# A two-layer decoder trunk: the recurrent mixer's chunks ordered by hand on four engines

## The chip, the cores and the metric

The kernel runs on one core of a Trainium2 chip. The metric is the device time of one execution, in microseconds (us). Times of "before" are the median of 3 runs, 2150.8 us (2145.18 to 2152.62). The engines are called as in the profile: PE is TensorE (PEld its weight loads), DVE VectorE, ACT ScalarE, POOL GpSimd, SP the engine whose queue issues most DMAs. One line of a timeline merges neighbouring instructions of one kind (x8: eight of them); a bracket at its end gives the idle time of the engine just before it and what ended that.

## The reference

x is 1024 tokens by 1024 features. Layer 0 mixes tokens with an mLSTM (4 heads, keys of 96, values of 192) beside a cross-attention over 256 memory tokens; one input projection feeds both, one output projection takes both. A SwiGLU feed-forward follows. Layer 1 does the same with a sliding-window attention. The change is in the mLSTM of layer 0:

```python
scores = einsum('bhcjd,bhcsd->bhcjs', qc, kc) * exp(dmat - m_row[..., None])   # decay mask, causal
num = einsum('bhcjs,bhcsv->bhcjv', scores, vc) + inter_w[..., None] * einsum('bhcjk,bhcvk->bhcjv', qc, C_st)
den = sum(scores, -1) + inter_w * einsum('bhcjk,bhck->bhcj', qc, n_st)
h = num / maximum(abs(den), exp(-m_row))[..., None]
C_new = decay * C + einsum('bhl,bhlv,bhlk->bhvk', w, v_c, k_c)                 # state, chunk after chunk
hm = hm * rsqrt(mean(hm * hm, -1) + EPS) * g_out * sigmoid(o)                  # norm per head, gate
```

The result does not depend on the length of a chunk; the kernel takes 128 tokens, so 8 chunks.

## The kernel before

All of it is one function, `trunk`, built with a scheduler that sets each engine's order and the semaphores. The program advances a nominal time with every matrix product that it emits (`line.now`). Side work is written as generators that `yield` a nominal delay; `line.poll` after each group of products emits what is due, and `line.need(key)` emits all that is left of a key. The scheduler may then move instructions against each other on an engine; inside `tc.manual_schedule` the written order of the named engines is kept.

Layer 0 starts with the memory's keys and values, then the input projection in six groups of columns (`ogm`, `q`, `k`, `v0`, `v1`, `o`; products `pa_...`). The weights of each group come in by SP's queue (`wa_k_raw`), ScalarE casts the high part (`wa_k_hi`, L237) and VectorE takes the rest (L238). During `q` the memory attention of the eight tiles runs as side work, and `gate_chain` computes the gates' running sums and maxima, from which come `iw`, `negm`, `ws`, `dec` and `ucol`; the row part of the decays goes to device memory (`r_spill`, 32 rows of 128). The sigmoid gates `o` are spilled too (`o_spill`).

Then comes the mixer, `mlstm_chunk(c)` (L1228). For each chunk of 128 tokens and 4 heads:

- SP loads the row decays, one row broadcast to all partitions (`dm`, L1233), POOL builds the weighted keys (`kw`, L1239) and adds the causal mask (L1246), ACT takes the exponential (L1257).
- PE transposes queries and keys (`pqk`), DVE and ACT copy one half each out of PSUM (`qkT`, L1254).
- PE multiplies scores (`psc`), DVE multiplies them by the decays (`sc`, L1262).
- PE multiplies keys by values, the growth of the state (`pu`), and DVE adds it to the decayed state (`state`, L1277).
- PE multiplies queries by the state before this chunk (`pi`) and scores by values (`pn`). ACT scales the first by `iw` (`num`, L1296), DVE adds the second (L1302).
- The norm: DVE forms the normaliser `den` in three small operations, a reciprocal last (L1312 to L1314); ACT takes the sum of squares of `num` times `den` (L1317, output `junk`); DVE, POOL (a power, L262) and DVE make the factor `r`; DVE multiplies values, factor and output gate into the page `v` (L1323).

Two chunks are alive at a time: chunk c starts chunk c + 2 after its sums. `dm`, `kw`, `qkT`, `state`, `num` have two buffers each, and `og`, the loaded gate, lies in the five shared pages (`xpage`). PSUM has eight banks, taken in turn.

`OutProjection.all` follows: it transposes pages 0, 4, 1 and 5 (`pt_mix`), ACT and DVE split each into two parts (`f`, L283 and L284), and the first products (`po`) use tiles 0 and 4, then 1 and 5; tiles 2, 6, 3 and 7 are transposed later. The weights' split parts are stored to device memory (`wst`) by SP. After that the feed-forward and layer 1 follow, with products in orders written by hand.

Of the kernel before, what the change touches and what calls it, by code (L numbers as in the profile page):

```python
# [9 lines left out]
F32 = mybir.dt.float32  # L10
# [110 lines left out]
def trunk(ctx: ExitStack, tc: tile.TileContext, a: dict, out: bass.AP):  # L121
# [430 lines left out]
    class OutProjection:  # L552
# [72 lines left out]
        def all(self, pages, first, early):  # L625
# [564 lines left out]
    for (nm, c0, n), after in zip(groups, groups[1:] + [None]):  # L1190
        for t0 in range(0, NT, 2):
# [27 lines left out]
    mneg = tp.tile([P, P], F32, name="mneg")  # L1219
    pool.memset(mneg, 0.0)  # L1220
    pool.affine_select(
        out=mneg, in_=mneg, pattern=[[1, P]], base=0, channel_multiplier=-1, compare_op=ALU.is_ge, fill=NEG
    )

    states = {}
    iw, nm_, ws, dec, ucol = (g_sb[n] for n in ("iw", "negm", "ws", "dec", "ucol"))

    def mlstm_chunk(c):  # L1228
        ck = slice(c * P, (c + 1) * P)
        va = vs[c][:, MEM_W:].rearrange("p (h d) -> p h d", h=HEADS)  # L1230

        dm = tp.tile([P, HEADS, P], F32, tag="dm", bufs=2, name=f"dm_{c}")
        nc.sync.dma_start(  # L1233
            out=dm.rearrange("p h n -> p (h n)"),
            in_=rd[c * HEADS : (c + 1) * HEADS, :].rearrange("h n -> (h n)").partition_broadcast(P),
        )
        if c < NT - 1:
            kw = tp.tile([P, HEADS, DQK], F32, tag="kw", bufs=2, name=f"kw_{c}")
            pool.tensor_tensor(  # L1239
                out=kw,  # L1240
                in0=qk[:, c, QK_W:].rearrange("p (h d) -> p h d", h=HEADS),
                in1=ws[:, c].unsqueeze(2).to_broadcast([P, HEADS, DQK]),
                op=ALU.mult,
            )
        yield 2.5 if c < 2 else 0.5
        pool.tensor_tensor(out=dm, in0=dm, in1=mneg.unsqueeze(1).to_broadcast([P, HEADS, P]), op=ALU.add)  # L1246

        qkT = tp.tile([DQK, 2, HEADS, P], F32, tag="qkT", bufs=2, name=f"qkT_{c}")
        for j in range(2):
            p = ps(f"pqk_{c}_{j}")  # L1250
            for h in range(HEADS):
                o = j * QK_W + h * DQK
                flip(p[:DQK, h * P : (h + 1) * P], qk[:, c, o : o + DQK])
            (act.copy if j else dve.tensor_copy)(qkT[:, j].rearrange("p h n -> p (h n)"), p[:DQK, :])  # L1254
        yield 1
        for h in range(HEADS):
            act.activation(dm[:, h], dm[:, h], AF.Exp, bias=ucol[:, c, h : h + 1])  # L1257
        psc = ps(f"psc_{c}")
        for h in range(HEADS):
            mm(psc[:, h * P : (h + 1) * P], qkT[:, 1, h], qkT[:, 0, h], True, True)  # L1260
        sc = tp.tile([P, HEADS, P], F32, tag="sc", bufs=2, name=f"sc_{c}")
        dve.tensor_tensor(out=sc, in0=psc.rearrange("p (h n) -> p h n", h=HEADS), in1=dm, op=ALU.mult)  # L1262

        if c < NT - 1:
            state = states.get(c - 1)
            new = states[c] = tp.tile([DQK, HEADS, DVA], F32, tag="state", bufs=2, name=f"state_{c}")
            for j in range(2):
                pu = ps(f"pu_{c}_{j}")
                for e_ in range(2):
                    h = 2 * j + e_  # L1270
                    mm(pu[:DQK, e_ * DVA : (e_ + 1) * DVA], kw[:, h], va[:, h], True, True)
                if c == 0:
                    dve.tensor_copy(new[:, 2 * j : 2 * j + 2].rearrange("p e d -> p (e d)"), pu[:DQK, : 2 * DVA])
                    continue
                for e_ in range(2):
                    h = 2 * j + e_
                    dve.scalar_tensor_tensor(  # L1277
                        out=new[:, h],
                        in0=state[:, h],
                        scalar=dec[:DQK, c, h : h + 1],  # L1280
                        in1=pu[:DQK, e_ * DVA : (e_ + 1) * DVA],
                        op0=ALU.mult,
                        op1=ALU.add,
                    )
        yield 2
        og = xpage(f"og_{c}")[:, :V_W]
        nc.sync.dma_start(out=og, in_=od[ck, :])
        num = tp.tile([P, HEADS, DVA], F32, tag="num", bufs=2, name=f"num_{c}")
        for j in range(2):
            nv = num[:, 2 * j : 2 * j + 2].rearrange("p e d -> p (e d)")  # L1290
            if c:
                pi = ps(f"pi_{c}_{j}")
                for e_ in range(2):
                    h = 2 * j + e_
                    mm(pi[:, e_ * DVA : (e_ + 1) * DVA], qkT[:, 0, h], states[c - 1][:, h], True, True)
                    act.mul(num[:, h], pi[:, e_ * DVA : (e_ + 1) * DVA], iw[:, c, h : h + 1])  # L1296
            pn = ps(f"pn_{c}_{j}")
            for e_ in range(2):
                h = 2 * j + e_
                mm(pn[:, e_ * DVA : (e_ + 1) * DVA], sc[:, h], va[:, h], True, True)  # L1300
            if c:
                dve.tensor_tensor(out=nv, in0=pn[:, : 2 * DVA], in1=nv, op=ALU.add)  # L1302
            else:
                dve.tensor_copy(nv, pn[:, : 2 * DVA])
            yield 0.5
        if c + 2 < NT:
            line.run(mlstm_chunk(c + 2), "mlstm")
        yield 0.5

        den, ss = (small([P, HEADS], n, bufs=2) for n in ("den", "ssh"))  # L1310
        dn = num[:, :, DV]
        dve.scalar_tensor_tensor(out=den, in0=dn, scalar=-1.0, in1=dn, op0=ALU.mult, op1=ALU.max)  # L1312
        dve.tensor_tensor(out=den, in0=den, in1=nm_[:, c], op=ALU.max)
        dve.reciprocal(den, den)  # L1314
        junk = xp.tile([P, 1024], BF16, tag="junk", bufs=1, name="junk")[:, :DV]
        for h in range(HEADS):
            act.activation(junk, num[:, h, :DV], AF.Square, scale=den[:, h : h + 1], accum_out=ss[:, h : h + 1])  # L1317
        yield 2
        r = rsqrt_mean(ss, DV, f"h_{c}", HEADS)
        dve.tensor_tensor(out=r, in0=r, in1=den, op=ALU.mult)  # L1320
        for h in range(HEADS):
            s = slice(h * DV, (h + 1) * DV)
            dve.scalar_tensor_tensor(  # L1323
                out=vs[c][:, MEM_W + h * DV : MEM_W + (h + 1) * DV],
                in0=num[:, h, :DV],
                scalar=r[:, h : h + 1],
                in1=og[:, s],
                op0=ALU.mult,
                op1=ALU.mult,
            )  # L1330
# [303 lines left out]
```

## Time and profile before

| | us |
|---|---|
| median of 3 runs (lowest, highest) | 2150.8 (2145.18, 2152.62) |
| the profiled execution | 2148.25 |
| its span, first to last instruction | 2146.5 |
| PE busy in the span | 2090.9 |
| from the first `pqk` to the first `po` | 295.29 to 369.76 |

All starts in the prediction are us from the span's first instruction. A busy time with its count divided gives the duration of one; where equal instructions follow each other without a gap, the start of the next row less the start of this gives what they cost the engine, since neighbours overlap a little. In the chain of waits each row holds only what that piece adds to the path.

### The profile page before, as it was taken

What the parts mean: (1) busy time and instruction counts of PE and PEld (TensorE: products, weight loads), DVE (VectorE), ACT (ScalarE), POOL (GpSimd) and SP (SyncE); (2) the same over time, 40 slices, a digit from 0 to 9 for tenths busy, and PEclk for the clock granted to TensorE, in tenths of its full rate; (3) what the DMA queues carried; (4) which work ended last, traced back from release to release, by engine and by line L of the source; (5) the groups of instructions that cost most, each with busy time, mean ns of one, the idle gap of its engine ahead of it and who ended that gap; (6) DMA issues with size and microseconds to landing.
All of it is one profiled execution on the core that took longest, in us unless ns stands there. A gap on an engine that the chain in (4) does not pass through costs nothing.

```text
span 2146.5 us, 30078 instructions
## 1 busy us (share of the span) xinstructions
PE 2090.9 (97%) x10628; PEld 1773.4 (83%) x10628; DVE 1281.9 (60%) x2449; ACT 1099.8 (51%) x2345; POOL 173.1 (8%) x277
## 2 busy tenths in 40 slices
PE   8999987999999999999999999999999999999998
PEld 7899977888888888888888888988888888888886
DVE  6332237577675766664585337757767667665556
ACT  6542236565545545354475336646555454544544
POOL 1000032022000000000012111001300000000002
PEclk9999998999999999999999999999999999999999
DMA  6111253693453544566674004049445445357667
GB/s 214 44 31 39 77 195 100 227 324 131 159 170 133 185 144 157 197 226 200 196 244 116 24 21 158 2 173 325 169 132 183 141 161 169 132 171 251 193 192 244
DMA packets 197814, 340.63 MB, mean 159 GB/s; under 512 B 23880, under 2 KB 79776, under 8 KB 197664
## 3 DMA queue, kind: packets, MB, share of 16 engines
q1 hardware_dynamic: 195360, 334.53, 47.1%
q10 hardware_dynamic: 2304, 4.20, 0.6%
q8 instruction: 83, 1.36, 0.3%
q14 instruction: 67, 0.55, 0.1%
HBM read 231.16 MB, written 104.35 MB: 156 GB/s over the span
## 4 chain that ended last, share of the span: by engine, by line
PE 79%; DVE 5%; issue 4%; ACT 3%; DMA 2%; POOL 1%; POOLq 0%; SPq 0%; DVEq 0%; ACTq 0%
PE fuu L186 11%; PE fgu L186 11%; PE fou L186 8%; PE po L186 7%; PE fud L186 6%; PE fgd L186 5%; PE fod L186 5%; PE foc L186 3%; PE fuc L186 3%; PE fgc L186 3%; PE pb_mq L186 2%; PE pb_q L186 2%; PE pa_v L186 2%; PE pov L186 2%; PE pa_k L186 2%
## 5 line engine op out<-in xcount | busy, mean ns | idle before, releaser
L944 DVE TENSOR_TENSOR so_lo<-so,so_hi 128x512 fp32r<-128x512 f32 x308 | 201.1, 690 | 156.3 <-ACT so_hi L943 156.1
L943 ACT CAST so_hi<-so 128x512 fp32r<-128x512 f32 x308 | 177.8, 619 | 196.3 <-PE fou L186 75.8
L186 PE MATMUL po<-wout_hi,f 128*128 128x512 f32 x512 | 162.0, 395 | 6.4 <-DVE f L284 6.4
L262 POOL TENSOR_TENSOR r<-v,neghalf 128x1 f32<-128x1 f32 (+1 forms) x76 | 59.2, 784 | 1099.0 <-DVE v L260 1070.0
L186 PE MATMUL fou<-so_lo,so_hi 128*128 128x512 f32 x352 | 137.3, 391 | 0.2
L186 PE MATMUL fou<-so_hi,so_lo 128*128 128x512 f32 x352 | 136.9, 389 | 0.0
L186 PE MATMUL fou<-so_hi,so_hi 128*128 128x512 f32 x352 | 135.2, 390 | 0.8 <-ACT so_hi L943 0.8
L186 PEld LDWEIGHTS po<-wout_hi,f 128*128 128x128 f32 x512 | 97.3, 190 | 26.7 <-DVE f L284 6.6
L186 PE MATMUL po<-wout_lo,f 128*128 128x512 f32 x256 | 100.8, 394 | 0.0
L186 PEld LDWEIGHTS fou<-so_lo,so_hi 128*128 128x128 f32 x352 | 66.1, 188 | 15.6 <-DVE so_lo L944 2.1
L186 PEld LDWEIGHTS fou<-so_hi,so_hi 128*128 128x128 f32 x352 | 66.0, 188 | 14.9 <-ACT so_hi L943 1.2
L186 PEld LDWEIGHTS fou<-so_hi,so_lo 128*128 128x128 f32 x352 | 66.1, 188 | 13.4
L699 ACT ACTIVATE wg<-wg,gcols 128x256 f32<-128x256 f32 x160 | 66.4, 499 | 13.5 <-DMA wg<-in_w_ffn_in 13.5
L710 DVE TENSOR_TENSOR t1u_lo<-wu,t1u_hi 128x512 fp32r<-128x512 f32 x22 | 15.2, 692 | 94.4 <-ACT t1u_hi L709 94.4
L186 PE MATMUL fod<-so_hi,so_hi 128*128 128x512 f32 x176 | 68.5, 389 | 0.0
L186 PE MATMUL fod<-so_lo,so_hi 128*128 128x512 f32 x176 | 68.5, 389 | 0.0
L186 PE MATMUL fod<-so_hi,so_lo 128*128 128x512 f32 x176 | 68.5, 389 | 0.0
L699 ACT ACTIVATE wu<-wu,gcols 128x256 f32<-128x256 f32 x160 | 66.5, 500 | 0.8 <-DMA wu<-in_w_ffn_in 0.8
L186 PE MATMUL pa_v<-wa_v_hi,h 128*128 128x384 f32 (+1 forms) x256 | 66.2, 339 | 0.0
L720 DVE TENSOR_TENSOR wo_raw<-wo_raw,wo_raw 128x512 f32<-128x512 f32 x88 | 60.6, 688 | 1.5
L186 PE MATMUL fgu<-f,t2g_hi 128*128 128x512 f32 (+1 forms) x176 | 53.5, 387 | 5.4 <-ACT gx L786 5.4
L186 PE MATMUL fuu<-f,t2u_hi 128*128 128x512 f32 x176 | 56.7, 403 | 0.3
(462 smaller groups left out, 5721.6 us busy)
## 6 DMA issues: line engine op xcount, KB each, us to landing
so<-sp SPq DMA_DIRECT2D x154, 256.0 KB, 3.1
wg<-in_w_ffn_in SPq DMA_DIRECT2D x44, 512.0 KB, 3.6
wo_raw<-in_w_ffn_out SPq DMA_DIRECT2D x88, 256.0 KB, 3.5
wu<-in_w_ffn_in SPq DMA_DIRECT2D x44, 512.0 KB, 4.2
tp<-wo_raw SPq DMA_DIRECT2D x88, 256.0 KB, 2.7
so<-tp SPq DMA_DIRECT2D x88, 256.0 KB, 3.3
so<-in_w_ffn_out SPq DMA_DIRECT2D x66, 256.0 KB, 3.7
sp<-ux SPq DMA_DIRECT2D x22, 512.0 KB, 3.8
```

Source lines behind the costliest of these rows:

```text
L186: pe.matmul(o, lhsT=lhsT, rhs=rhs, start=start, stop=stop, **kw)
L262: pool.tensor_tensor(out=r, in0=v, in1=neghalf[:, :width], op=ALU.pow)
L699: act.activation(v, v, AF.Copy, scale=g)
L710: dve.tensor_tensor(out=lo, in0=v, in1=h.bitcast(F32), op=ALU.subtract)
L720: dve.tensor_tensor(out=r[o], in0=r[x_], in1=r[y_], op=ALU.add)
L943: act.copy(h, v)
L944: dve.tensor_tensor(out=lo, in0=v, in1=h.bitcast(F32), op=ALU.subtract)
```

## The change

The mixer becomes a loop of ten rounds, i from -2 to 7, inside `tc.manual_schedule` for PE, DVE, ACT and POOL. A round holds four chunks at once: transposes of chunk i + 2, scores and state of i + 1, sums of i, norm of i - 1, and the gates of i - 2 (two heads each in its middle and at its end). Loads and masks run ahead: the decays of i + 4 are loaded, those of i + 3 masked, those of i + 2 exponentiated. Buffers grow to three (`qkT`, `state`, `num`, `og`) and four (`dm`, `den`, `ssh`); `og` and `num` have pages of their own except in the last two chunks.

The norm loses its reciprocal: ACT squares `num` itself, and the factor is (mean of squares + EPS den²) to the power -1/2. The third small operation on `den` is now EPS den² (L1362 of the changed kernel), and the two around the power become one ahead of it (L1371).

The memory attention gets a pool of its own, which is given back after the `v1` columns; the mask and the four `dm` buffers take that room, and decays of chunks 0 to 2 are written there (`first_decays`). The norms of the last two chunks are side work (`m_end`, key "ends"), needed before `keep(0)` in the output projection.

```diff
@@ OutProjection.all
             self.tiles(0, (0, 4))
+            line.need("ends")
             self.keep(0)
...
+    def first_decays():
+        for c in range(4):
+            decay_load(c)
+        yield 6
+        for c in range(3):
+            decay_mask(c)
+            if c < 2:
+                state_keys(c)
+            yield 1.5
+            if c < 2:
+                decay_exp(c)
...
-    line.need("gates", "mem0")
+        elif nm == "v1":
+            line.need("gates", "mem0")
+            mem_cm.__exit__(None, None, None)
...
+            line.run(first_decays(), "decay", 4)
+    line.need("decay")
...
-        dve.reciprocal(den, den)
+        dve.scalar_tensor_tensor(out=den, in0=den, scalar=EPS, in1=den, op0=ALU.mult, op1=ALU.mult)
...
+    def m_scale(c):
+        den, ss = vals[c]
+        dve.scalar_tensor_tensor(out=den, in0=ss, scalar=1.0 / DV, in1=den, op0=ALU.mult, op1=ALU.add)
+        pool.tensor_tensor(out=ss, in0=den, in1=neghalf[:, :HEADS], op=ALU.pow)
...
+    def m_end(c):
+        yield 1
+        for h in range(HEADS):
+            m_square(c, h)
+        yield 2
+        m_scale(c)
+        yield 1.5
+        m_gate(c, range(HEADS))
+
+    with tc.manual_schedule(engines={mybir.EngineType[e] for e in ("PE", "DVE", "Activation", "Pool")}):
+        pn1 = None
+        for i in range(-2, NT):
+            ends = 0 <= i - 1 < NT - 2
+            if 0 <= i < NT:
+                m_load(i)
+            if 4 <= i + 4 < NT:
+                decay_load(i + 4)
+            flips = m_flip(i + 2) if i + 2 < NT else None
+            if pn1:
+                m_add(i - 1, 1, pn1)
+            if flips:
+                dve.tensor_copy(*flips[0])
+            if i >= 1:
+                m_normaliser(i - 1)
+            if 0 <= i - 2 < NT - 2:
+                m_gate(i - 2, (0, 1))
+            if 0 <= i + 1 < NT:
+                psc = m_scores(i + 1)
...
+            if ends:
+                m_square(i - 1, 0)
+            if flips:
+                act.copy(*flips[1])
+            if ends:
+                for h in range(1, HEADS):
+                    m_square(i - 1, h)
+            if 0 <= i + 1 < NT - 1:
+                m_state(i + 1, m_growth(i + 1))
+            if ends:
+                m_scale(i - 1)
+            if 2 <= i + 2 < NT - 1:
+                state_keys(i + 2)
+            if i >= 0:
+                if 3 <= i + 3 < NT:
+                    decay_mask(i + 3)
+                pi, pn = m_sums(i, 0)
+                if pi:
+                    m_scaled(i, 0, pi)
+                m_add(i, 0, pn)
+                if i + 2 < NT:
+                    decay_exp(i + 2, (0, 1))
...
+            if 0 <= i - 2 < NT - 2:
+                m_gate(i - 2, (2, 3))
+        m_add(NT - 1, 1, pn1)
+        m_normaliser(NT - 1)
+        m_gate(NT - 3, range(HEADS))
+    for c in (NT - 2, NT - 1):
+        line.run(m_end(c), "ends", 0.5 + c - NT + 2)
```

What this makes of the engines' order is shown at three places. The first is DVE in the middle of the mixer; `v` is the page that the gates write, `num` the sums, `sc` the decayed scores. Before:

```order
L1302 TENSOR_TENSOR num_3008<-pn_0_3014,num_3008 128x386
L1277 SCALAR_TENSOR_TENSOR state_2986<-state_2955,dec,pu_0_2987 96x193 x2
L1277 SCALAR_TENSOR_TENSOR state_2986<-state_2955,dec,pu_1_2992 96x193 x2
L1302 TENSOR_TENSOR num_3008<-pn_1_3023,num_3008 128x386
L1302 TENSOR_TENSOR num_3029<-pn_0_3035,num_3029 128x386
L1312 SCALAR_TENSOR_TENSOR den<-num_3008 128x4
L1313 TENSOR_TENSOR den<-den,negm 128x4
L1314 RECIPROCAL den<-den 128x4
L1302 TENSOR_TENSOR num_3029<-pn_1_3048,num_3029 128x386
L1254 COPY qkT_3063<-pqk_0_3064 96x512
```

and in one round of the change:

```order
L1352 TENSOR_TENSOR num_2979<-pn_1_3049,num_2979 128x386
L1408 COPY qkT_3063<-pqk_0_3064 96x512
L1360 SCALAR_TENSOR_TENSOR den<-num_2979 128x4
L1361 TENSOR_TENSOR den<-den,negm 128x4
L1362 SCALAR_TENSOR_TENSOR den<-den 128x4
L1378 SCALAR_TENSOR_TENSOR v_616<-num_2903,ssh,og_2902 128x192 x2
L1416 TENSOR_TENSOR sc_3088<-psc_3083,dm_2855 128x512
L1321 SCALAR_TENSOR_TENSOR state_3105<-state_3025,dec,pu_0_3099 96x193 x2
L1321 SCALAR_TENSOR_TENSOR state_3105<-state_3025,dec,pu_1_3100 96x193 x2
L1371 SCALAR_TENSOR_TENSOR den<-ssh,den 128x4
L1352 TENSOR_TENSOR num_3059<-pn_0_3118,num_3059 128x386
L1378 SCALAR_TENSOR_TENSOR v_616<-num_2903,ssh,og_2902 128x192 x2
```

Where two chunks' steps stood next to each other, every round now has each step once, with four chunks' buffers side by side.

The second place is ACT ahead of the `k` columns; `mpT` belongs to the memory attention's last tile, `qk` is the copied projection. Before:

```order
L492 COPY mpT_7_1_1599<-mpt_7_1_1594 128x512
L237 ACTIVATE wa_k_hi<-wa_k_raw,gcols 128x384 x4
L1173 COPY qk<-pa_q_1558 128x384
L237 ACTIVATE wa_k_hi<-wa_k_raw,gcols 128x384
L1173 COPY qk<-pa_q_1559 128x384
```

and in the change:

```order
L492 COPY mpT_7_1_1602<-mpt_7_1_1597 128x512
L237 ACTIVATE wa_k_hi<-wa_k_raw,gcols 128x384 x3
L1175 ACTIVATE dm_2520<-dm_2520,ucol 128x128
L237 ACTIVATE wa_k_hi<-wa_k_raw,gcols 128x384
L1213 COPY qk<-pa_q_1561 128x384
L237 ACTIVATE wa_k_hi<-wa_k_raw,gcols 128x384
L1213 COPY qk<-pa_q_1562 128x384
L1175 ACTIVATE dm_2520<-dm_2520,ucol 128x128 x3
L1175 ACTIVATE dm_2522<-dm_2522,ucol 128x128 x4
```

The exponentials of chunks 0 and 1 (`dm_2520`, `dm_2522`), written in the program behind the `v1` columns, stand here, the first of them between the sixth and the seventh cast of the `k` weights; on SP their loads stand ahead of the v weights.

The third place is DVE at the mixer's end; `v_903` is chunk 5's page, `v_1069` chunk 6's, `v_1066` and `v_1074` chunks 6 and 7 of before. Before:

```order
L260 TENSOR_SCALAR v_3375<-ssh 128x4
L1320 TENSOR_TENSOR r_3377<-r_3377,den 128x4
L1323 SCALAR_TENSOR_TENSOR v_1066<-num_3315,r_3377,og_3313 128x192 x4
L260 TENSOR_SCALAR v_3384<-ssh 128x4
L1320 TENSOR_TENSOR r_3386<-r_3386,den 128x4
L1323 SCALAR_TENSOR_TENSOR v_1074<-num_3327,r_3386,og_3325 128x192 x4
L284 TENSOR_TENSOR f_3400<-pt_mix_0_0_3401,f_3400 128x512
```

and in the change:

```order
L1352 TENSOR_TENSOR num_3339<-pn_1_3361,num_3339 128x386
L1371 SCALAR_TENSOR_TENSOR den<-ssh,den 128x4
L1360 SCALAR_TENSOR_TENSOR den<-num_3339 128x4
L1361 TENSOR_TENSOR den<-den,negm 128x4
L1378 SCALAR_TENSOR_TENSOR v_1069<-num_3292,ssh,og_3291 128x192
L1362 SCALAR_TENSOR_TENSOR den<-den 128x4
L1378 SCALAR_TENSOR_TENSOR v_903<-num_3217,ssh,og_3216 128x192 x4
L1371 SCALAR_TENSOR_TENSOR den<-ssh,den 128x4
L1378 SCALAR_TENSOR_TENSOR v_1069<-num_3292,ssh,og_3291 128x192 x2
L284 TENSOR_TENSOR f_3387<-pt_mix_0_0_3388,f_3387 128x512
```

Chunk 7's gates now come after the `f` subtractions of pages 0, 4, 1 and 5. Chunk 5's four gates appear here although the round before had them already: the loop's last round has i - 2 = 5, and the line after the loop issues them once more. Behind these rows each engine's order is that of before.

More of the change, by code (lines that the diff above doesn't have):

```diff
@@ L1218, in trunk @@
     tp = tp0.pool
[L1219 to L1235, printed above, removed]
-        )
[L1237 to L1248, printed above, removed]
@@ new lines, in trunk, with m_load, m_flip @@
+    qkTs, scs_, states, nums, ogs, vals = {}, {}, {}, {}, {}, {}
+    def m_load(c):
+        late = c >= NT - 2
+        ogs[c] = xpage(f"og_{c}")[:, :V_W] if late else tp.tile([P, V_W], F32, tag="og", bufs=3, name=f"og_{c}")
+        nums[c] = (
+            xpage(f"num_{c}")[:, : HEADS * DVA]
+            if late
+            else tp.tile([P, HEADS * DVA], F32, tag="num", bufs=3, name=f"num_{c}")
+        )
+        nc.sync.dma_start(out=ogs[c], in_=od[c * P : (c + 1) * P, :])
+    def m_flip(c):
+        qkT = qkTs[c] = tp.tile([DQK, 2, HEADS, P], F32, tag="qkT", bufs=3, name=f"qkT_{c}")
+        pqk = [ps(f"pqk_{c}_{j}") for j in range(2)]
@@ L1249, in mlstm_chunk @@
         for j in range(2):
-            p = ps(f"pqk_{c}_{j}")
             for h in range(HEADS):
                 o = j * QK_W + h * DQK
[L1253 to L1257, printed above, removed]
+                flip(pqk[j][:DQK, h * P : (h + 1) * P], qk[:, c, o : o + DQK])
@@ L1264, in mlstm_chunk @@
[L1264 to L1288, printed above, removed]
-        for j in range(2):
[L1290 to L1297, printed above, removed]
+        return psc
@@ L1311, in mlstm_chunk, with m_sums @@
-        dn = num[:, :, DV]
+                dve.scalar_tensor_tensor(
+                    out=new[:, h],
+                    in0=states[c - 1][:, h],
+                    scalar=dec[:DQK, c, h : h + 1],
+                    in1=pus[j][:DQK, e_ * DVA : (e_ + 1) * DVA],
+                    op0=ALU.mult,
+                    op1=ALU.add,
+                )
+    def m_sums(c, j):
+        va, sc, qkT, pi = m_values(c), scs_[c], qkTs[c], None
+        if c:
+            pi = ps(f"pi_{c}_{j}")
+            for e_ in range(2):
+                h = 2 * j + e_
+                mm(pi[:, e_ * DVA : (e_ + 1) * DVA], qkT[:, 0, h], states[c - 1][:, h], True, True)
+        pn = ps(f"pn_{c}_{j}")
+        for e_ in range(2):
+            h = 2 * j + e_
+            mm(pn[:, e_ * DVA : (e_ + 1) * DVA], sc[:, h], va[:, h], True, True)
+        return pi, pn
@@ new lines, in m_scaled, with m_add, m_normaliser @@
+    def m_scaled(c, j, pi):
+        for e_ in range(2):
+            h = 2 * j + e_
+            act.mul(nums[c][:, h * DVA : (h + 1) * DVA], pi[:, e_ * DVA : (e_ + 1) * DVA], iw[:, c, h : h + 1])
+    def m_add(c, j, pn):
+        v = nums[c][:, 2 * j * DVA : 2 * (j + 1) * DVA]
+        if c:
+            dve.tensor_tensor(out=v, in0=pn[:, : 2 * DVA], in1=v, op=ALU.add)
+        else:
+            dve.tensor_copy(v, pn[:, : 2 * DVA])
+    def m_normaliser(c):
+        den = small([P, HEADS], "den", bufs=4)
+        dn = nums[c].rearrange("p (h d) -> p h d", h=HEADS)[:, :, DV]
```

89 lines of the change are left out of this document (65 added, 24 removed).

## The prediction

> **What bounds the kernel now.** The page comes first: TensorE is busy for nearly the whole span, so only what shortens TensorE's own row of work, or its waits, counts.
>
> ```profile
> span 2146.5 us, 30078 instructions
> PE 2090.9 (97%) x10628; PEld 1773.4 (83%) x10628; DVE 1281.9 (60%) x2449; ACT 1099.8 (51%) x2345; POOL 173.1 (8%) x277
> ```
>
> The profiled execution took 2148.25 us, 1.75 us more than its span. The change touches the recurrent mixer, so I cut its stretch out by windows: from the first chunk's transposes to the fifth score product (L186, `psc`), on to the ninth, and on to the first product of the output projection. Columns: stretch, its length, busy time (and instructions) of PE, PEld, DVE, ACT, POOL, granted clock, DMA share, GB/s.
>
> ```profile
> 295.29:317.44 22.15, 15.57 (x90) 13.90 (x88) 10.77 (x22) 11.10 (x32) 11.47 (x12) 0.85 0.86 296
> 317.44:349.58 32.14, 27.37 (x161) 25.91 (x161) 24.92 (x68) 19.68 (x64) 12.21 (x11) 0.89 0.41 136
> 349.58:369.76 20.18, 12.61 (x91) 11.72 (x89) 13.97 (x46) 13.53 (x44) 4.04 (x4) 0.95 0.24 78
> ```
>
> Here no engine is full: PE is busy 55.55 of 74.47 us, and at a granted clock of 0.85 to 0.95. PE's timeline gives the milestones and the long waits.
>
> ```profile
> 295.29 1.04 PE L193 MATMUL pqk<-ident,qk 128*96 128x128 f32 x8
> ...
> 299.65 1.04 PE L193 MATMUL pqk<-ident,qk 128*96 128x128 f32 x8
> 304.70 2.08 PE L186 MATMUL psc<-qkT 96*128 96x128 f32 x8 [4.01 <-ACT qkT L1254]
> ...
> 317.44 1.16 PE L186 MATMUL psc<-qkT 96*128 96x128 f32 x8 [0.51 <-ACT qkT L1254]
> ...
> 349.58 1.12 PE L186 MATMUL psc<-qkT 96*128 96x128 f32 x8
> ...
> 369.76 0.80 PE L186 MATMUL po<-wout_hi,f 128*128 128x512 f32 x1 [6.35 <-DVE f L284]
> ```
>
> Three stretches: 22 us until chunk 2's scores; then four chunks (2 to 6) in 32.14 us, 8.0 us each; then 20 us to the projection, of which the last 6.35 us are a wait for chunk 7's norm.
>
> **The change, part by part.** Its instructions are almost those of before; their order is new. So I price a round of the new order on each engine, then follow the path. VectorE's starts, row to next row, are the cost of each operation:
>
> ```profile
> 333.62 0.68 DVE L1254 COPY qkT<-pqk 96x512 f32<-96x512 f32 x1
> 334.22 0.15 DVE L1313 TENSOR_TENSOR den<-den,negm 128x4 f32<-128x4 f32 x1
> ...
> 350.79 0.69 DVE L1262 TENSOR_TENSOR sc<-psc,dm 128x512 f32<-128x512 f32 x1 [0.31 <-PE psc L186]
> 351.40 1.39 DVE L1277 SCALAR_TENSOR_TENSOR state<-state,dec,pu 96x193 f32<-96x193 f32 x4
> 352.71 0.16 DVE L260 TENSOR_SCALAR v<-ssh 128x4 f32<-128x4 f32 x1
> ...
> 354.20 1.41 DVE L1323 SCALAR_TENSOR_TENSOR v<-num,r,og 128x192 f32<-128x192 f32 x4
> 355.52 0.17 DVE L260 TENSOR_SCALAR v<-ssh 128x4 f32<-128x4 f32 x1
> ...
> 358.33 1.02 DVE L1302 TENSOR_TENSOR num<-pn,num 128x386 f32<-128x386 f32 x2
> 359.38 0.17 DVE L1312 SCALAR_TENSOR_TENSOR den<-num 128x4 f32<-128x4 f32 x1
> ...
> 360.07 1.03 DVE L1302 TENSOR_TENSOR num<-pn,num 128x386 f32<-128x386 f32 x2
> ```
>
> Copy 0.60, score 0.61, four state updates 1.31, four gates 1.32, two adds 1.05, three small normaliser operations 0.69, and the new scale step, of the small ones' kind, 0.2: 5.8 us a round on VectorE. TensorE's price is in the chain of waits, where it runs back to back.
>
> ```profile
> 347.99 1.75 PE pqk L193 x16
> 349.74 0.96 PE psc L186 x8
> 350.70 1.32 PE pu L186 x8
> ```
>
> Eight transposes are 0.88, scores 0.96, growth 1.32; the two sums have 193 columns like growth, so I take 1.32 for each: 5.8 us too. ScalarE:
>
> ```profile
> 302.90 1.28 ACT L1257 ACTIVATE dm<-dm,ucol 128x128 f32<-128x128 f32 x4
> ...
> 359.62 0.75 ACT L1296 ACTIVATE num<-pi,iw 128x193 f32<-128x193 f32 x2 [0.37 <-PE pi L186]
> 360.27 0.44 ACT L1317 ACTIVATE junk<-num,den 128x192 bf16<-128x192 f32 x1
> ...
> 360.84 0.46 ACT L1317 ACTIVATE junk<-num,den 128x192 bf16<-128x192 f32 x1
> ```
>
> A square costs 0.57 (360.27 to 360.84), two scalings 0.65, four exponentials 1.28, a copy about as VectorE's: 2.3 + 1.3 + 1.3 + 0.6 = 5.5 us. With three engines at 5.5 to 5.8, a round without any collision is about 5.9. But GpSimd works in every round, and the trace shows who collides with it:
>
> ```profile
> 324.65 1.26 POOL L1246 TENSOR_TENSOR dm<-dm,mneg 128x512 f32<-128x512 f32 x1 [0.17 <-POOL r L262]
> ...
> 336.36 0.83 POOL L1239 TENSOR_TENSOR kw<-qk,ws 128x384 f32<-128x384 f32 x1 [7.48 <-PE pu L186]
> ...
> 338.66 1.16 POOL L262 TENSOR_TENSOR r<-v,neghalf 128x4 f32<-128x4 f32 x1 [0.36 <-DVE v L260]
> ```
> ```profile
> 324.72 2.40 DVE L1323 SCALAR_TENSOR_TENSOR v<-num,r,og 128x192 f32<-128x192 f32 x4
> ...
> 338.54 1.41 DVE L1323 SCALAR_TENSOR_TENSOR v<-num,r,og 128x192 f32<-128x192 f32 x4
> ```
>
> Four gates that began just behind a mask (`dm`, 1.26 us) took 2.40 instead of 1.41: the first stood still until the mask ended. Beside a power (`r`) they took their 1.41. So I count the mask as a stop for VectorE's operations that read SBUF alone (normaliser, gates), and the power as none. In the new order GpSimd does power, keys, mask after each scale step: 1.02 + 0.83 + 1.26, with three hand-overs of 0.07 (quoted below) 3.3 us after the scale. VectorE meanwhile has an add, two gates, an add and a copy, 0.5 + 0.66 + 0.5 + 0.6 = 2.3, and comes to the normaliser 1.0 early. It then needs 0.69 + 0.66 (gates) + 0.61 + 1.31 + 0.2 = 3.5 to the next scale. Round: 3.3 + 3.5 = **6.8 us**.
>
> The Trainium skill (SBUF — State Buffer, § Who interferes with whom) says that a VectorE instruction with two SBUF inputs contends with any GpSimd instruction that reads SBUF, the first to start holding the pair to its end. For the mask the trace agrees (2.40 against 1.41); for the power the 338.54 row does not show it (1.41). By that rule the power too would stop two gates.
>
> Now the path. **Lead-in**: chunk 0's and 1's masks and exponentials have moved ahead of the mixer, so after the unchanged point 299.65 (growth of chunk 0 done, next transposes) round 0 needs only PE's 0.88 + 0.96 + 1.32 + 1.32 = 4.5, to 304.1, and chunk 2's scores start at 305.0 instead of 317.44: **-12.4**. The table load of ScalarE falls into round 0, where chunk 2's exponentials are not needed before 306. **Rounds**: four chunks at 6.8 instead of 32.14 in all: 27.2, **-4.9**. They reach chunk 6's scores at 332.2; the last scale step before the end phase (chunk 4's) is at 335.4, 3.2 behind. **End**: add, gates, add 1.7 (337.1); ScalarE's four squares of chunk 5 2.3 (339.4); scalings of chunk 6 and VectorE's add, with two gates between, 2.5 (341.9); then in the order in which ScalarE holds them two squares 1.2, two scalings 0.65, two squares 1.2, two scalings 0.65 and the add 0.5 (346.1). VectorE: scale 0.2, power with hand-overs 1.1, one gate of chunk 6 and its neighbour 0.4, four gates of chunk 5 that the change issues a second time 1.3, scale of chunk 7 0.2, two gates 0.7, the first `f` subtraction 0.7: 350.7, and the projection starts at 350.8. From chunk 6's scores that is 18.6 instead of 20.18: **-1.6**. Of the chain that ended the stage before, the last norm's power and gates no longer stand there:
>
> ```profile
> 362.76 0.07 issue
> 362.83 1.02 POOL r L262
> ...
> 366.88 1.42 DVE v L1323 x4
> ```
>
> The reciprocal was one small operation and is replaced by one: nothing. Chunk 7's power and gates go behind the `f` evictions, under the first projection pair; were that cover gone, they would cost 1.0 + 1.4 = 2.4. SP's queue now carries three decay loads ahead of the v weights and a fourth among them, and ScalarE's queue one exponential ahead of the last two `wa_k` casts:
>
> ```profile
> 144.42 1.75 PE mpo L186 x16
> ...
> 150.39 33.28 PE pa_k L186 x192
> ```
> ```profile
> DMA to landing us min/median/max: 3.2/4.1/6.0
> ```
>
> The load waits for the memory attention's end (146.2), lands by 152.2 at the slowest row of decays, mask and exponential 1.7, cast and subtraction 1.3: 155.2. PE needs that seventh slice after 36 of the 192 products of 0.173: 156.6. So I take 0, with a slack of 1.4; each us of landing beyond that costs one. In the mixer a load has more than a round, 7 us or more against 6.0, before its mask: 0. An earlier load frees nothing that PE waits for under `pa_k`, so this part has no gain; its bounds are 0 and +2.
>
> Sum: -12.4 - 4.9 - 1.6 = -18.9. On the profiled 2148.25 that gives 2129.3; the median of the three runs, 2150.8, is 2.5 above it, so I forecast a median of **2131.9**.
>
> **The rivals.** (a) The pace of before returns: rounds stay at 8.0, since each engine's queue now waits in a fixed order. Against it: each mask and exponential now stands a round or more ahead of its score; for it: VectorE was already 24.92 of 32.14 busy. Four rounds cost 4.8 more: 2136.7. (b) The power stops the gates too. Two gates then wait from 0.5 after the scale to 1.1, and push keys and mask: 0.6 a round, 2.4: 2134.3. The Trainium skill page above is the ground for that rule; the 338.54 row speaks against. (c) The change does not do what it says: the decays, once moved under the k columns, hold ScalarE's casts there, and TensorE waits as long as it gains. That takes landings of some 25 us against 6.0: about 2150. (d) Slower: the granted clock. Where PE waits 4.01, eight scores took 2.08 instead of 0.96. If rounds with waits keep the clock at half, a round is PE's 11.6: five of them, 24 more; lead-in and last rounds add 10: 2166. It decides once about 25 of these 34 come true. Against it, the middle stretch held 0.89 with PE busy for 85%, which the new round equals.
>
> No collision at all, rounds of 5.9, gives -3.6: 2128.3. That is the forecast's own lower end, 8.0 the upper.
>
> **How the numbers follow.** Forecast 0.70, (a) 0.15, (b) 0.08, (c) 0.04, (d) 0.03. Runs of this kernel lie from 2145.18 to 2152.62, so 0.3%, 6.5 us, is about what can be told from no change; faster are the first three cases, 0.93, the same is (c), slower (d). The range goes from 2128.3 less the 5 that spread and a shorter end allow, 2123, to (a) with 2 for the loads and 2 for the spread, 2141.
>
> **What would show it.** In the changed profile: chunk 2's scores 9.7 us after the first transposes, not 22; score rows 6.8 apart; gates or normaliser of over 1 us beside a mask, none beside a power; the first projection product 55.5 us after the first transposes, with a wait of 3 to 7; and no new wait in `pa_k`. Wrong would be score rows 8 or more apart, a granted clock under 0.8 in the rounds, or a gap before `pa_k` or `pa_v`.

## The result and the profile after

The changed kernel takes 2125.38 us (median of 4 runs, 2124.24 to 2130.15), the kernel before, run beside it, 2151.62 (4 runs, 2145.18 to 2152.62). The ratio is 0.9896, with a 95% interval of 0.9879 to 0.9912 (the quotient of the two medians is 0.9878): faster by about 1%, against a forecast of 2131.9 with a range of 2123 to 2141. Its profiled execution took 2125.09 us, 23.2 less than the 2148.25 of before, where the sum of the prediction had 18.9 less.

The page of the changed kernel, as before: TensorE has 10.3 us less of busy time (2080.6 against 2090.9) with as many instructions; 7.8 of them are gone from the mixer's stretch (47.8 against 55.6), whose granted clock is now 0.99 to 1.00 and was 0.85 to 0.95.

```profile
span 2123.0 us, 30079 instructions
...
PE 2080.6 (98%) x10628; PEld 1764.2 (83%) x10628; DVE 1280.8 (60%) x2445; ACT 1096.6 (52%) x2345; POOL 174.3 (8%) x277
```

The same three stretches by windows (length; busy time and instructions of PE, PEld, DVE, ACT, POOL; granted clock; DMA share; GB/s): first transposes to chunk 2's scores, on to chunk 6's, on to the projection.

```profile
296.48:305.89 9.41, 9.41 (x73) 9.13 (x72) 7.65 (x16) 5.92 (x13) 5.02 (x4) 1.00 0.89 267
305.89:328.73 22.84, 22.84 (x162) 22.63 (x161) 20.82 (x59) 18.61 (x67) 10.08 (x10) 1.00 0.73 257
328.73:346.94 18.21, 15.54 (x107) 14.45 (x105) 17.00 (x53) 13.70 (x52) 6.91 (x7) 0.99 0.21 72
```

In the first two TensorE is busy all the time. PE's timeline shows score rows 5.71 us apart, with no wait before chunk 6's; waits of some length come only ahead of the projection.

```profile
296.48 1.91 PE L193 MATMUL pqk<-ident,qk 128*96 128x128 f32 x16
...
305.89 1.06 PE L186 MATMUL psc<-qkT 96*128 96x128 f32 x8
...
311.60 1.06 PE L186 MATMUL psc<-qkT 96*128 96x128 f32 x8
...
328.73 1.06 PE L186 MATMUL psc<-qkT 96*128 96x128 f32 x8
330.15 1.55 PE L186 MATMUL pu<-v,kw 128*96 128x193 f32 x8 [0.36 <-POOL kw L1180]
...
344.65 1.61 PE L193 MATMUL pt_mix<-ident,v 128*128 128x128 f32 x8 [1.55 <-DVE v L1378]
...
346.94 0.79 PE L186 MATMUL po<-wout_hi,f 128*128 128x512 f32 x1 [0.67 <-DVE f L284]
```

So the account, on the profiled executions: lead-in 22.15 to 9.41, -12.7; rounds 32.14 to 22.84, -9.3; end 20.18 to 18.21, -2.0; the first transposes 1.2 later (296.48 against 295.29); from the projection's first product to the last instruction 1776.1 against 1776.7, -0.7; outside the span 2.1 against 1.75, +0.3. Together -23.2. Nothing is given back behind the mixer.

VectorE does not keep TensorE's pace. Rows of its rounds in the changed kernel (L1371 is the scale step, L1360 the first normaliser operation, L1378 the gates):

```profile
308.99 0.15 DVE L1371 SCALAR_TENSOR_TENSOR den<-ssh,den 128x4 f32<-128x4 f32 x1
...
317.82 0.77 DVE L1360 SCALAR_TENSOR_TENSOR den<-num 128x4 f32<-128x4 f32 x1
...
321.47 0.16 DVE L1371 SCALAR_TENSOR_TENSOR den<-ssh,den 128x4 f32<-128x4 f32 x1
...
323.74 1.22 DVE L1360 SCALAR_TENSOR_TENSOR den<-num 128x4 f32<-128x4 f32 x1
324.99 0.16 DVE L1361 TENSOR_TENSOR den<-den,negm 128x4 f32<-128x4 f32 x1
...
325.28 0.75 DVE L1378 SCALAR_TENSOR_TENSOR v<-num,ssh,og 128x192 f32<-128x192 f32 x2
...
327.85 0.15 DVE L1371 SCALAR_TENSOR_TENSOR den<-ssh,den 128x4 f32<-128x4 f32 x1
...
328.39 0.73 DVE L1378 SCALAR_TENSOR_TENSOR v<-num,ssh,og 128x192 f32<-128x192 f32 x2
...
334.24 0.15 DVE L1371 SCALAR_TENSOR_TENSOR den<-ssh,den 128x4 f32<-128x4 f32 x1
```

and GpSimd's beside them:

```profile
321.71 1.20 POOL L1372 TENSOR_TENSOR ssh<-den,neghalf 128x4 f32<-128x4 f32 x1 [3.15 <-PE pi L186]
322.89 0.82 POOL L1180 TENSOR_TENSOR kw<-qk,ws 128x384 f32<-128x384 f32 x1
323.67 1.26 POOL L1171 TENSOR_TENSOR dm<-dm,mneg 128x512 f32<-128x512 f32 x1
328.08 1.22 POOL L1372 TENSOR_TENSOR ssh<-den,neghalf 128x4 f32<-128x4 f32 x1 [3.14 <-PE pn L186]
```

The first normaliser operation, 0.15 to 0.18 us where it is free, starts at 323.74, just behind the mask's start at 323.67, and ends at 324.96 with the mask (324.93). Two gates under a power take 0.73 (328.39), and 0.75 where GpSimd rests (325.28). VectorE's period, from scale to scale (321.47 to 327.85), is 6.38 us, TensorE's 5.71. So VectorE falls behind: its scale comes 3.1 us after chunk 2's scores (308.99 and 305.89) and 5.5 us after chunk 6's (334.24 and 328.73). TensorE feels this first at 330.15, where it waits 0.36 us for GpSimd's keys, which are issued behind scale and power. Two questions follow: what lets TensorE run ahead, and which part of the change the 24 us between transposes and projection belong to.

### The profile page after: what moved, and what is told of

Read it like the earlier page. It is cut to its first block, busy times and chain, and to the rows that moved or that the text cites. A ratio compares the mean times of both kernels' runs of the same rounds, so it can differ in the third digit from the quotient of the medians.

```text
span 2123.0 us, 30079 instructions
## 1 busy us (share of the span) xinstructions
PE 2080.6 (98%) x10628; PEld 1764.2 (83%) x10628; DVE 1280.8 (60%) x2445; ACT 1096.6 (52%) x2345; POOL 174.3 (8%) x277
## 3 DMA queue, kind: packets, MB, share of 16 engines
q1 hardware_dynamic: 195360, 334.53, 47.8%
## 4 chain that ended last, share of the span: by engine, by line
PE 82%; DVE 6%; DMA 3%; ACT 2%; issue 2%; POOL 1%; POOLq 0%; SPq 0%; DVEq 0%; ACTq 0%
PE fuu L186 11%; PE fgu L186 11%; PE fou L186 9%; PE fud L186 6%; PE fod L186 5%; PE fgd L186 5%; PE po L186 5%; PE pa_v L186 3%; PE foc L186 3%; PE fuc L186 3%; PE fgc L186 3%; PE pb_mq L186 2%; PE pb_q L186 2%; PE pa_o L186 2%; PE pov L186 2%
## 5 line engine op out<-in xcount | busy, mean ns | idle before, releaser
L262 POOL TENSOR_TENSOR r<-v,neghalf 128x1 f32<-128x1 f32 x68 | 51.8, 767 | 1071.2 <-DVE v L260 1045.4
L700 ACT ACTIVATE wg<-wg,gcols 128x256 f32<-128x256 f32 x160 | 66.6, 500 | 12.4 <-DMA wg<-in_w_ffn_in 12.4
```

Of the source, the lines that this page charges most:

```text
L262: pool.tensor_tensor(out=r, in0=v, in1=neghalf[:, :width], op=ALU.pow)
L700: act.activation(v, v, AF.Copy, scale=g)
```

## The experiments

The theory after the result: GpSimd's mask stops VectorE, which falls behind; buffers let TensorE run on, so that in eight chunks the lag shows only at the end; the lead-in's gain is the early decays'. The rival: TensorE alone sets the stage, and who is late on the other engines matters to nobody.

Single runs differ behind the mixer by more than most of these edits are worth (from the first `po` to the last instruction 1775 to 1785 us over all runs), so each is measured by the way from the first transposes to the first `po`. All starts are from PE's timeline; the last column is one execution, that of the profile.

| kernel | to chunk 2's scores | chunk 2's to 6's | chunk 6's to `po` | the way | time |
|---|---|---|---|---|---|
| before | 22.15 | 32.14 | 20.18 | 74.47 | 2148.25 |
| changed | 9.41 | 22.84 | 18.21 | 50.46 | 2125.09 |
| masks twice | 9.42 | 24.78 | 20.14 | 54.34 | 2128.22 |
| blank fills | 9.42 | 22.84 | 18.22 | 50.48 | 2132.81 |
| normaliser behind state | 9.42 | 22.84 | 17.25 | 49.51 | 2124.90 |
| no repeat | 9.41 | 22.84 | 16.43 | 48.68 | 2125.58 |
| late decays | 13.54 | 23.94 | 18.30 | 55.78 | 2127.94 |
| norms ahead | 9.42 | 22.84 | 20.12 | 52.38 | 2131.61 |
| two buffers, qkT and state | 9.41 | 35.17 | 24.20 | 68.78 | 2143.50 |
| two buffers, qkT alone | 9.56 | 35.18 | 24.28 | 69.02 | 2146.01 |
| reciprocal, no repeat | 9.41 | 24.03 | 19.92 | 53.36 | 2130.57 |
| behind state, no repeat | 9.42 | 22.84 | 15.47 | 47.73 | 2122.46 |
| old order, early decays | 16.47 | 29.26 | 20.17 | 65.90 | 2141.61 |
| old order, three buffers | 21.77 | 31.43 | 19.55 | 72.75 | 2146.71 |

**Does the mask stop VectorE, and does that matter?** The mask twice:

```diff
                 if 3 <= i + 3 < NT:
                     decay_mask(i + 3)
+                    decay_mask(i + 3)
```

> Each decay mask of the mixer's rounds (chunks 3 to 7) is issued twice on GpSimd, with no change of the result. Measured is the way from the first transposes to the projection's first product, 50.46 us in the changed kernel. Theory (a mask stops VectorE's operations that read SBUF alone; VectorE's rounds then take 6.4 us, and buffers of three take up the lag): the normaliser now stands still for up to 2.5 us instead of 1.2, VectorE's rounds go to about 7.6 us, TensorE can no longer run ahead of them, and the way takes 55 to 57 us. Rival (GpSimd has time to spare, the mask matters to nobody): at most 0.5 us longer.

The way is 3.9 us longer, 54.34, a little under the range. VectorE's rows of this kernel, and PE's:

```profile
325.76 1.24 DVE L1360 SCALAR_TENSOR_TENSOR den<-num 128x4 f32<-128x4 f32 x1
327.04 0.16 DVE L1361 TENSOR_TENSOR den<-den,negm 128x4 f32<-128x4 f32 x1
327.24 1.12 DVE L1362 SCALAR_TENSOR_TENSOR den<-den 128x4 f32<-128x4 f32 x1
...
333.11 1.24 DVE L1360 SCALAR_TENSOR_TENSOR den<-num 128x4 f32<-128x4 f32 x1
```
```profile
317.33 1.06 PE L186 MATMUL psc<-qkT 96*128 96x128 f32 x8
...
323.35 1.06 PE L186 MATMUL psc<-qkT 96*128 96x128 f32 x8
...
330.69 1.06 PE L186 MATMUL psc<-qkT 96*128 96x128 f32 x8
333.14 1.55 PE L186 MATMUL pu<-v,kw 128*96 128x193 f32 x8 [1.39 <-POOL kw L1180]
```

Each mask stops one operation (1.24 and 1.12), VectorE's period is 7.35 (325.76 to 333.11). TensorE takes 5.71 for the first rounds, then 6.02, then 7.34: it runs ahead until it has to wait for the keys, which GpSimd writes behind VectorE's scale (1.39 at 333.14), and then has VectorE's period. That is less than the expected cost because the first rounds were free.

The control: GpSimd as long at work, but without reading.

```diff
                     decay_mask(i + 3)
+                    for _ in range(4):
+                        pool.memset(blank, 0.0)
```

> Instead of a second mask, GpSimd fills a tile that nobody reads four times behind each mask: it is as long busy or longer, but reads nothing of SBUF. Theory (GpSimd's reads stop VectorE): the normaliser's durations stay as in the changed kernel, at most 1.3 us, and the way from the first transposes to the projection stays at 50.5 us, within 0.7. Rival (what matters is GpSimd's time in the round, so that keys and power come late): 55 us or more, as with the masks twice.

The way is 50.48, the changed kernel's. GpSimd's rows, then VectorE's beside them:

```profile
329.26 1.28 POOL L1171 TENSOR_TENSOR dm<-dm,mneg 128x512 f32<-128x512 f32 x1
330.49 2.26 POOL L1437 MEMSET blank<- 128x512 f32 x4
```
```profile
329.31 1.25 DVE L1361 SCALAR_TENSOR_TENSOR den<-num 128x4 f32<-128x4 f32 x1
330.60 0.16 DVE L1362 TENSOR_TENSOR den<-den,negm 128x4 f32<-128x4 f32 x1
330.80 0.16 DVE L1363 SCALAR_TENSOR_TENSOR den<-den 128x4 f32<-128x4 f32 x1
```

The mask stops the first operation (1.25); 2.26 us of fills stop nothing (0.16). It is not GpSimd's time. The Trainium skill (SBUF — State Buffer, § Who interferes with whom) says that a VectorE instruction with two SBUF inputs contends with a GpSimd instruction that reads SBUF and not with one that only writes it: mask and fills agree, with these numbers; the power, which also reads, does not (two gates in 0.73 under it).

Now the stop taken away, by order: normaliser and two gates move behind the state updates, so that the mask falls on operations that read PSUM.

```diff
-            if i >= 1:
-                m_normaliser(i - 1)
-            if 0 <= i - 2 < NT - 2:
-                m_gate(i - 2, (0, 1))
...
                 m_state(i + 1, m_growth(i + 1))
+            if i >= 1:
+                m_normaliser(i - 1)
+            if 0 <= i - 2 < NT - 2:
+                m_gate(i - 2, (0, 1))
```

> On VectorE the normaliser and the two gates of a round move behind the four state updates, so that the mask falls beside operations that read PSUM. Theory (the mask's stop costs VectorE some 1.1 us in each of the later rounds, and VectorE ends the stage): no normaliser of over 0.3 us, VectorE's rounds at 5.8 us, and the way from the first transposes to the projection 2 to 2.7 us shorter, 47.8 to 48.5. Rival (TensorE alone sets the rounds, and the end is the chain of the last norms, which no mask touches): 50.5, within 0.5.

The stop is gone: no first operation of a normaliser in the rounds takes over 0.16, and VectorE's period is 5.71 (scales at 321.25 and 326.96 below), TensorE's, with waits of 0.32 in it. The way is shorter, but by 1.0 instead of 2 to 2.7.

```profile
321.25 0.15 DVE L1370 SCALAR_TENSOR_TENSOR den<-ssh,den 128x4 f32<-128x4 f32 x1
...
325.81 0.15 DVE L1360 SCALAR_TENSOR_TENSOR den<-num 128x4 f32<-128x4 f32 x1
...
326.96 0.16 DVE L1370 SCALAR_TENSOR_TENSOR den<-ssh,den 128x4 f32<-128x4 f32 x1
```

In the chain of waits of this kernel ScalarE's scalings, exponentials and squares stand (331.4 to 334.4) where the stopped normaliser stood in that of the changed one; then the chain runs over VectorE as before. A row of each, the changed kernel's first:

```profile
330.19 1.18 DVE den L1360
```
```profile
332.74 0.74 ACT num L1347 x2
```

So about half of the lag was hidden: without it, ScalarE is next.

**The end.** The gates that are issued a second time, dropped:

```diff
         m_normaliser(NT - 1)
-        m_gate(NT - 3, range(HEADS))
```

> The four gates of chunk 5 that the change issues a second time are dropped. Theory (from the last rounds to the projection the chain runs over VectorE): 1.3 us less, the way from the first transposes takes 49.1. Rival (VectorE waits there for GpSimd's power of chunk 6 anyway, so that the repeat is hidden): 50.5, within 0.4.

1.8 us shorter, more than the four gates' 1.3, because the order shifts with them: one more gate of chunk 6 and chunk 7's scale now also go behind the first `f` subtractions. And the last norms ahead of the projection, as they were:

```diff
         line.run(m_end(c), "ends", 0.5 + c - NT + 2)
+    line.need("ends")
```

> The last two norms' power and gates are issued ahead of the f subtractions of the projection, as before the change. Theory (chunk 7's power and gates are hidden under the first projection pair and would cost 1.0 + 1.4 there): the projection begins 2.4 us later, 52.9 us after the first transposes. Rival (the power is hidden behind the gates that come first; only the four gates count): 1.4 later, 51.9.

1.9 us longer, between the two: to put the last norms under the first projection pair is worth 1.9, not 2.4.

**The lead-in.** First decays back behind the input columns (moved, otherwise unchanged):

```diff
-            line.run(first_decays(), "decay", 4)
-    line.need("decay")
     sc_["h"].close()
...
+    line.run(first_decays(), "decay")
+    line.need("decay")
```

> The loads, masks and exponentials of the first decays go back to behind the last input columns, as before the change; all else stays changed. Theory (the lead-in's gain is these operations' move, under the k columns they cost nothing): chunk 2's scores come 17 us or more after the first transposes instead of 9.4, the way to the projection takes 57 us or more instead of 50.5, and the stretch ahead of the first transposes stays within 0.5 of its length. Rival (the lead-in is shorter because of the new order of the rounds, and the decays would be ready in time from either place): 9.4 and 50.5 within 1.

The way is 5.3 us longer, 55.78 where 57 or more was expected, and chunk 2's scores come after 13.54 us, not 17 or more: the theory's numbers fail. So does its last point: the first transposes start 1.2 us earlier than in the changed kernel's profile (295.27 against 296.48), where 0.5 was allowed; the kernels with early decays, though, differ among themselves by more than that (294.50 to 296.81). The decays explain 4.1 us of the lead-in, not 12.4. The same part alone, in the old order (the helpers of the change, called from `mlstm_chunk`):

```diff
+            line.run(first_decays(), "decay", 4)
...
-        dm = tp.tile([P, HEADS, P], F32, tag="dm", bufs=2, name=f"dm_{c}")
-        nc.sync.dma_start(...)
+        if c >= 4:
+            decay_load(c)
+        dm = dms[c]
...
+        if c >= 3:
+            decay_mask(c)
...
+        if c >= 2:
+            decay_exp(c)
```

> The kernel before, with one part of the change alone: four decay tiles, the first loads, masks and exponentials under the k columns. The prediction's lead-in term gave all of 12.4 us to this move. Theory after the run with late decays (the move is worth 4 to 5 us, the rest of the lead-in belongs to the new order): chunk 2's scores 16 to 18 us after the first transposes instead of 22.15, and the projection 68 to 70 us after them instead of 74.5. Rival (the prediction's attribution): scores at 9.7 to 11 and the projection at 62 to 64.

Chunk 2's scores come after 16.47, as expected, the projection after 65.90, which lies between the two expectations; the rounds have gained 2.9 too, which no theory had. PE's rows of this kernel show what still holds the lead-in:

```profile
311.15 0.59 PE L186 MATMUL pi<-state,qkT 96*128 96x193 f32 x2 [2.17 <-ACT num L1335]
...
312.24 1.06 PE L186 MATMUL psc<-qkT 96*128 96x128 f32 x8
...
314.45 1.05 PE L186 MATMUL psc<-qkT 96*128 96x128 f32 x8
```

It is no longer the decays but the old order: chunk 2's scores stand behind the sums of chunks 0 and 1, and those wait for ScalarE's scalings, here 2.17. So of the lead-in's 12.7 us the decays' move makes 4.1 to 5.7, by whether the order is new or old, and the order the other 7 to 8.6. That the rest is the order follows by exclusion: without the third `qkT` buffer or with the reciprocal the lead-in stays at 9.56 and 9.41 (table).

**The third buffer.** The first run had transposed queries and keys (`qkT`) and `state` at two, the second `qkT` alone:

```diff
-        qkT = qkTs[c] = tp.tile([DQK, 2, HEADS, P], F32, tag="qkT", bufs=3, name=f"qkT_{c}")
+        qkT = qkTs[c] = tp.tile([DQK, 2, HEADS, P], F32, tag="qkT", bufs=2, name=f"qkT_{c}")
```

> The transposed queries and keys and the state get two buffers instead of three, in the same order. Theory (TensorE keeps 5.7 us a round while VectorE takes 6.4, because three buffers let it run ahead): TensorE now waits in every round, rounds of about 7 us, and the way from the first transposes to the projection is 6 to 9 us longer. Rival (VectorE is never in TensorE's way; 5.7 is what the new order gives on any buffers): at most 1 us longer.

> Only the transposed queries and keys get two buffers instead of three; the state keeps three. Theory (the copy into the third buffer is what lets VectorE and ScalarE work on while TensorE is at the sums of an older chunk): the whole loss of the run with both at two comes back, 68.8 us from the first transposes to the projection, within 1.5, and rounds of 9.5 us. Rival (the state's buffer holds VectorE's updates until TensorE has read the old state): 51 us or less.

68.78 and 69.02: 18 us longer, at least twice the 6 to 9 that the first run was expected to lose, and all of it by `qkT`. The later rounds are 9.5 us, longer than the 8.0 of before. VectorE's copy of the run with `qkT` alone at two, and PE's rows:

```profile
328.62 0.69 DVE L1408 COPY qkT<-pqk 96x512 f32<-96x512 f32 x1 [4.12 <-PE pi L186]
```
```profile
331.69 1.06 PE L186 MATMUL psc<-qkT 96*128 96x128 f32 x8
334.56 1.55 PE L186 MATMUL pu<-v,kw 128*96 128x193 f32 x8 [1.82 <-POOL kw L1180]
...
338.76 0.92 PE L186 MATMUL pn<-v,sc 128*128 128x193 f32 x4 [0.67 <-ACT qkT L1422]
...
340.71 0.64 PE L193 MATMUL pqk<-ident,qk 128*96 128x128 f32 x4 [0.60 <-ACT num L1347]
341.19 1.06 PE L186 MATMUL psc<-qkT 96*128 96x128 f32 x8
```

The copy stands at the head of a round on VectorE, and with two buffers it may not write until TensorE has read chunk i's queries for the last time, at that round's end. Everything that VectorE has in the round queues behind it for 4.12 us, ScalarE's own half of the copy waits likewise (4.76), and TensorE then waits for keys, copies and scalings. In the old order the same buffers do little:

```diff
-        qkT = tp.tile([DQK, 2, HEADS, P], F32, tag="qkT", bufs=2, name=f"qkT_{c}")
+        qkT = tp.tile([DQK, 2, HEADS, P], F32, tag="qkT", bufs=3, name=f"qkT_{c}")
...
-            new = states[c] = tp.tile([DQK, HEADS, DVA], F32, tag="state", bufs=2, name=f"state_{c}")
+            new = states[c] = tp.tile([DQK, HEADS, DVA], F32, tag="state", bufs=3, name=f"state_{c}")
```

> The kernel before, with three buffers for the transposed queries and keys and for the state, and nothing else. Theory (in the old order a chunk's transposes are issued behind the sums of the chunk two before it, when two buffers are free again; the third is worth something only with the new order): 74.5 us from the first transposes to the projection, within 1. Rival (the third buffer brings the rounds' gain by itself): 70 or less, rounds of 7 us or less instead of 8.0.

72.75: 1.7 less, just beyond the 1 allowed, and far from 70. The third buffer brings nothing much by itself; the new order cannot do without it.

**The norm.** The reciprocal back, to be compared with "no repeat", 48.68:

```diff
-        dve.scalar_tensor_tensor(out=den, in0=den, scalar=EPS, in1=den, op0=ALU.mult, op1=ALU.mult)
+        dve.reciprocal(den, den)
...
-        act.activation(junk, nums[c][...], AF.Square, accum_out=...)
+        act.activation(junk, nums[c][...], AF.Square, scale=vals[c][0][:, h : h + 1], accum_out=...)
...
+            dve.tensor_tensor(out=r, in0=r, in1=vals[c][0], op=ALU.mult)
```

> The norm gets its reciprocal back (squares scaled by it, the factor multiplied by it; the repeated gates are dropped, since they would scale twice), to be compared with the kernel that only drops the repeat. Theory of the prediction (one small operation for one): the same way from the first transposes to the projection, within 0.5. Rival (a square that takes the denominator as its scale waits for VectorE, and ScalarE's copy of the keys behind it waits too, so that VectorE's lag reaches TensorE): 1 to 3 us longer, TensorE's rounds over 6 us.

53.36, 4.7 longer, more than the rival had. ScalarE's, VectorE's and GpSimd's rows of this kernel:

```profile
326.46 0.46 ACT L1367 ACTIVATE junk<-num,den 128x192 bf16<-128x192 f32 x1 [1.69 <-DVE ssh L1377]
...
328.99 0.71 ACT L1347 ACTIVATE num<-pi,iw 128x193 f32<-128x193 f32 x2
```
```profile
329.74 0.56 DVE L1352 TENSOR_TENSOR num<-pn,num 128x386 f32<-128x386 f32 x1 [0.45 <-PE pqk L193]
330.21 1.31 DVE L1380 SCALAR_TENSOR_TENSOR v<-num,ssh,og 128x192 f32<-128x192 f32 x2
```
```profile
330.36 0.95 POOL L1180 TENSOR_TENSOR kw<-qk,ws 128x384 f32<-128x384 f32 x1
```

ScalarE's first square waits 1.69 us for the denominator (the profile names L1377, the multiplication of the factor of the chunk before, which stands right behind the reciprocal on VectorE and ends 0.04 us after it), so its copy and scalings come late. VectorE's add, which the profile puts down to PE, starts at 329.74, 0.04 behind the end of ScalarE's two scalings (328.99 to 329.70); it has waited 0.45 for them. That pushes two gates under GpSimd's keys, and they take 1.31 instead of 0.74. VectorE and ScalarE now wait for each other once a round, 6.72 us long by the two score rows of the later rounds (322.82 and 329.54); 1.2 of the 4.7 us are lost there, 3.5 in the end. The run does not separate this waiting from what else comes back with the reciprocal: the multiplication of the factor on VectorE, and squares that take 0.45 us instead of 0.36.

**Both savings at once,** no repeat and normaliser behind the state:

> Both savings at once: normaliser and gates behind the state updates, and no repeated gates. If the two are independent (1.0 and 1.8 us in the runs that made one each), the way from the first transposes to the projection is 47.7 us instead of 50.46, and the time about 2.7 us less than the changed kernel's, near 2122.5; if the wait for the last norms' power sets the end in both, only the larger remains: 48.7. Either is within the spread of single runs, so the way is the measure and the time a bound.

```profile
296.81 1.91 PE L193 MATMUL pqk<-ident,qk 128*96 128x128 f32 x16
...
344.54 0.50 PE L186 MATMUL po<-wout_hi,f 128*128 128x512 f32 x1 [0.83 <-DVE f L284]
```

The way is 47.73, so the savings add. The time is 2122.46 (median of 5 runs, 2121.06 to 2128.57), the ratio to before 0.9885 with an interval of 0.9868 to 0.9903. The changed kernel's 0.9896 lies in it: the 2.7 us are shown by the traces, not by the times.

## Why the prediction held, and where it failed

The measured median lies 6.5 us under the forecast. The terms miss by 4.3 us in sum, the rounds alone by 4.4. The range holds the result because its lower end left 5 us below the case without collision, for the spread and a shorter end; no mechanism of the forecast led there, so that part is luck.

**The lead-in** was right in size (-12.4, measured -12.7; 9.41 us against 9.7) and wrong in its cause. It priced the new order's round 0 on TensorE alone, which is right, and credited the masks and exponentials that had moved ahead. They make 4.1 to 5.7 us; the rest is the order.

**The rounds** were mis-sized: 6.8 us predicted, -4.9; 5.71 measured, -9.3. Two steps failed. First, VectorE's own period came out at 6.38, not 6.8. GpSimd's part was as predicted: 3.3 from the scale's end to the mask's (321.63 to 324.93). From there to the end of the next scale it takes 3.0 (324.96 to 328.00), where the prediction had 3.5: it counted all three small normaliser operations there, 0.69, while the first had ended with the mask and the other two take 0.32 up to the gates (324.96 to 325.28). Second and larger, it took VectorE's period for TensorE's. VectorE had a lead to lose: while its lag grew from 3.1 to 5.5 us, TensorE did not wait until after chunk 6's scores, and with a longer stop (masks twice) it still ran at 5.71 until that lead was gone. The prediction never priced the third `qkT` buffer, which stands in the change in plain sight and which this needs: with two, VectorE's copy itself waits for TensorE, and a round is 9.5 us. The case without collision (5.9 a round, 2128.3), the prediction's lower end, is near to what TensorE did, though the collision is there.

**The end** was right in size, 18.2 against 18.6, but not in its path. The prediction went over ScalarE's squares and scalings from 337.1 to 346.1; in the changed kernel's chain of waits no row of ScalarE stands from chunk 6's scores on (328.73): it runs over VectorE up to chunk 6's power at 342.62. So that the sizes agree is partly luck. The wait ahead of the projection, put at 3 to 7 us, is 1.55 and 0.67. Of the end's pieces, the last norms under the projection are worth 1.9, where 2.4 was given, and the repeated gates cost 1.8, where 1.3 was counted.

**The norm** was priced at nothing, one small operation for one. That was a count of operations and not of waits: with the reciprocal the squares need the denominator, and with its multiplication and longer squares the way is 4.7 us longer. The gain of it sits inside the terms for rounds and end.

**The k columns** were priced at 0, bounds 0 to +2. PE is busy throughout them in the changed kernel (by windows, 140 to 190 us after the start):

```profile
140.00:190.00 50.00, 50.00 (x299) 49.93 (x298) 11.70 (x21) 19.60 (x46) 5.99 (x5) 1.00 0.30 85
```

From 190 to the first transposes it has no gap either (106.48 of 106.48 us). The first transposes start at 294.50 to 296.81 in eleven kernels with early decays, mean 296.0, and at 295.27 to 295.50 in three without, mean 295.4: some 0.7 later, which runs this far apart do not settle.

**The rivals.** Rounds at 8.0 (a) did not come; without the third `qkT` buffer they were 8.8 in the mean (35.18 for four). The power as a stop (b) is refuted by the gates under it, 0.73 to 0.74 in each round. ScalarE's casts held in the k columns (c): no wait there. The clock at half (d): 1.00 in the rounds.

## What to carry to other kernels

A round of a pipeline has a period on each engine, and the slowest of them is the kernel's only if the others cannot run ahead: over a few rounds, work out how large a lead there is to lose before taking the longest period as the pace, and look at what a copy at the head of a queue must wait for, which the number of buffers decides. Price an operation that goes by who had to wait for its result, not by its duration; and where two parts of a change could earn the same microseconds, do each alone, in the old order and in the new.

## What the runs showed of the hardware

GpSimd's mask (128x512, two inputs in SBUF, 1.26 us) and its keys (128x384, 0.8 to 0.95 us) stopped VectorE's operations whose inputs all lie in SBUF, when these began under them, until they ended; operations that read PSUM beside them kept their time, as did operations beside fills. A power over 128x4 stopped none, but itself took 1.20 to 1.22 us in three rounds of the changed kernel and 1.01 to 1.05 in the other five; the runs do not show why.

In the mixer's rounds a square of 128x192 without a scale operand took 0.35 to 0.37 us (changed kernel), one that takes its scale from a column of SBUF 0.44 to 0.46 (the kernel before and the one with the reciprocal).

Behind the same two waits, 1.55 and 0.67 us, the first 25 us of the projection had a granted clock of 0.94 in the changed kernel and of 1.00 in the one with late decays: what the clock does after a wait is not set by that wait alone.
